# A hybrid decoder layer on one core: for twelve weight chunks of the down projection a DMA makes the low part

## The chip, the cores and the metric

The kernel runs on one core of a Trainium2 chip. A core has TensorE for matrix products, VectorE (DVE in the profile), ScalarE (ACT) and GpSimd (POOL) for elementwise work, SyncE (SP), which here only issues loads, and sixteen DMA engines that all queues share. The engines run side by side, each works through its own instructions in order, and they wait for each other through semaphores. The metric is the time of the whole program on the device in microseconds; lower is better.

## The reference

One layer works on 256 tokens of width 2048: a mixer of two recurrent branches, cross-attention, and a gated feed-forward network with a short causal convolution. The change concerns the last product of it, the down projection from 8192 to 2048.

```python
def conv_glu_ffn(h, w_up, conv_w, conv_b, w_down):
    u = h @ w_up
    uc = conv_b + sum(conv_w[j] * shift_right(u, CONV_WIDTH - 1 - j) for j in range(CONV_WIDTH))
    gate, up = split_cols(uc, (D_FF, D_FF))
    return (jax.nn.gelu(gate, approximate=True) * up) @ w_down
...
    x = x + rms_norm(y, mix_post_norm[l])
...
    x = x + rms_norm(cross_attention(h, m, xattn_wq[l], xattn_wkv[l], xattn_wo[l]), xattn_post_norm[l])
    h = rms_norm(x, ffn_pre_norm[l])
    x = x + rms_norm(conv_glu_ffn(h, ffn_w_up[l], ffn_conv_w[l], ffn_conv_b[l], ffn_w_down[l]), ffn_post_norm[l])
```

All inputs and the result are float32.

## The kernel before

**Split products.** TensorE reads its operands as `float32r`, which keeps fewer bits than float32. So each float32 matrix is split into a high part, the value rounded to `float32r`, and a low part, the value minus the high part, and a product becomes three: x high by w high, x low by w high, x high by w low. Splitting a weight chunk takes a cast by ScalarE (`wh`, line 448 in `Feed.hi`) and a subtraction by VectorE (`wl = raw - wh`, line 520 in `Feed.lo`).

**Chunks and buffers.** A weight chunk is 512 KB: 128 partitions by 1024 float32. `Feed` lists the chunks of all blocks in the order of their use (`src`). `dma` loads them with SP's queue into `raw` tiles (four buffers), `hi` makes `wh` tiles and `lo` makes `wl` tiles (five buffers each). A buffer comes free when the last reader of its earlier contents is done: for `raw` that is the subtraction, for `wh` and `wl` the matmuls of the chunk five places earlier.

**The down projection** is two blocks of kind `tm`, one for each half of the 2048 output columns, with 64 chunks each. A chunk holds 128 of the 8192 inputs and 1024 output columns. It is multiplied into four PSUM banks of 128 tokens by 512 columns, which makes 4 x 3 = 12 matmuls, by `tm_products` (line 524): for each bank the three products one after the other. The activations are split too (`as`, in `asplit`): a ScalarE cast and a VectorE subtraction for every two chunks.

**Pairs.** At six places of each block (`SEVEN`: 12, 20, 30, 38, 48, 56 and 10, 18, 28, 36, 46, 54) two chunks k and k + 1 are multiplied together by a scheme with seven block products in place of eight, so 21 matmuls in place of 24 (`seven_products`). Their weights have buffers of their own (`sraw`, loaded by `pair_loads`), and sums of the blocks are prepared in small steps in the six chunks before (`prepare`, `ahead_of_pairs`). The step of the loop that does a pair sets `skip`, so the loop runs no step for chunk k + 1.

**The order** of every engine's instructions is written out by `run`/`work`. In the step of chunk i it first makes sure of the splits up to `i + 1` (`feed.lo(i + 1 + pair)`), calls the activations' split (`b["xs"](k)`), then the splits up to `i + 3`, the loads up to `i + 7`, and then issues the matmuls of chunk i. `side.half()` gives other work, such as the evaluation of a finished block, its turn on VectorE and ScalarE. POOL has nothing to do in the down projection until its last microseconds.

Of the kernel before, what the change touches and what calls it, by code (L numbers as in the profile page):

```python
# [11 lines left out]
AF = mybir.ActivationFunctionType  # L12
ALU = mybir.AluOpType
AX = mybir.AxisListType

P = 128
# [138 lines left out]
def _layer(ctx, tc, nc, d, dbg):  # L155
    act, dve = Meter(nc.scalar, 200.0, 0.83), Meter(nc.vector, 130.0, 1.04)
    pool, pe, sp = nc.gpsimd, nc.tensor, nc.sync
# [32 lines left out]
    def mm(out, lhsT, rhs, start=True, stop=True):  # L190
        pe.matmul(out, lhsT, rhs, start=start, stop=stop, skip_group_check=True)  # L191
# [63 lines left out]
    def turns(ap):  # L255

        return ap.rearrange("p (a b) -> p b a", a=2)
# [25 lines left out]
    class Stat:  # L283


        def __init__(self, name, tag="ysb1", sq="au", home=None):
            self.name, self.tag, self.sq, self.home = name, tag, sq, home
            self.rc = cp.tile([P, 2], F32, name=name + "_c")
            self.n = 0
            self.done = False  # L290
# [89 lines left out]
    blocks = []  # L380
# [10 lines left out]
    class Feed:  # L391
        def __init__(self):
            a, g = blocks[0]["srcs"], blocks[1]["srcs"]
            self.src = a[:LEAD] + [c for p in zip(a[LEAD:], g) for c in p] + g[len(a) - LEAD:]
            self.src += [s for b in blocks[2:] for s in b["srcs"]]
            n, self.pairs, self.preps = sum(len(b["srcs"]) for b in blocks[:2]), {}, []
            for b in blocks[2:]:
                if b["seven"]:
                    for k in b["seven"]["at"]:
                        self.pairs[n + k], self.pairs[n + k + 1] = 0, 1  # L400
                        self.preps.append([n + k - 6, self.prepare(n + k, k), n + k, []])
                n += len(b["srcs"])
            self.raw, self.st, self.nd, self.ns, self.nl, self.nop = {}, {}, 0, 0, 0, 0
# [38 lines left out]
        def hi(self, upto):  # L442
            while self.ns <= min(upto, len(self.src) - 1):
                self.dma(self.ns)
                r = self.raw[self.ns]
                wh = self.staged("wh", r)
                for o, v in self.pieces(self.ns, wh, r):
                    nc.scalar.copy(o, v)  # L448
                self.st[self.ns] = [wh, None]
                self.ns += 1  # L450

        def prepare(self, c, k):
# [61 lines left out]
        def lo(self, upto):  # L514
            self.hi(upto)
            while self.nl <= min(upto, len(self.src) - 1):
                r = self.raw.pop(self.nl)
                wl = self.staged("wl", r)
                for o, v, h in self.pieces(self.nl, wl, r, self.st[self.nl][0]):
                    nc.vector.tensor_sub(o, v, h)  # L520
                self.st[self.nl][1] = wl
                self.nl += 1

    def tm_products(o, t, c, wx, first, last):
        wh, wl, xh, xl = wx
        t = slice(t // P * P, t // P * P + P)
        wh, wl = (turns(w[:, c:c + 512]) for w in (wh, wl))
        mm(o, xh[:, t], wh, start=first, stop=False)
        mm(o, xl[:, t], wh, start=False, stop=False)
        mm(o, xh[:, t], wl, start=False, stop=last)  # L530

    def seven_products(b, banks, ci, w0h, w0l, w1h, w1l):
        sv = b["seven"]
# [35 lines left out]
    def run():  # L569
        feed = Feed()  # L570
# [3 lines left out]
        i = 0  # L574
        pend = []

        def work(b):
# [6 lines left out]
            if b["wide"]:  # L584
                banks = [b["pool"]("fm", [P, 2, S]) for _ in range(nm)]
            elif b["kind"] == "fm":
                banks = [b["pool"]("fm", [P, 2, S]) for _ in range((nm + 1) // 2 * (1 + b["two"]))]
            else:
                banks = [b["pool"]("tm")[:, 0:min(b["cols"], 512)] for _ in range(2 * -(-b["cols"] // 512))]
            nk = sum(s.shape[1] for s in b["srcs"]) // (1 + b["two"])  # L590
            k = 0
# [4 lines left out]
            for ci, s in enumerate(b["srcs"]):  # L596
                if skip:
                    skip = False
                    continue
                join = b["seven"] and ci - b["seven"]["at"][-1]  # L600
                second = b["two"] and ci % 2
                if second:
                    k -= s.shape[1]
                if b["pre"]:
                    b["pre"](ci, feed)
                pair = 1 if b["seven"] and ci in b["seven"]["at"] else 0
                feed.lo(i + 1 + pair)
                side.half(True)
                side.more = lambda: feed.hi(i + 2)
                ahead = b["xs"](k)  # L610
                if b["seven"]:
                    feed.pair_loads(i)
                feed.lo(i + 3 + pair)
                feed.dma(i + 7 + pair)
                if b["seven"]:
                    feed.ahead_of_pairs(i)
                if b["seven"]:
                    if join >= 2:
                        if join == 2:
                            b["seven"]["joins"] = join_sums(b["seven"])  # L620
                        next(b["seven"]["joins"], None)
                wh, wl = feed.st.pop(i)
                later = []
                if b["seven"] and ci in b["seven"]["at"]:
                    seven_products(b, banks, ci, wh, wl, *feed.st.pop(i + 1))
                    k, i, skip = k + 2, i + 2, True
                    yield
                    continue
                for kj in range(s.shape[1]):
                    xh, xl = b["xs"](k) if kj else ahead  # L630
                    first, last = k == 0, k == nk - 1
                    if b["wide"]:
                        xw = b["xw"](k).rearrange("p h (a b) -> p h b a", a=2)
                        for m in range(nm):
                            a, c = (w[:, kj, m * P:(m + 1) * P] for w in (wh, wl))
                            mm(banks[m].rearrange("p h s -> p (h s)"), a, xw, start=first, stop=False)
                            mm(banks[m][:, 0], c, turns(xh), start=False, stop=last)
                    elif b["kind"] == "fm":
                        xh, xl = turns(xh), turns(xl)
                        for m in range(nm):  # L640
                            r = min(P, b["cols"] - m * P)
                            o = banks[second * 2 + m // 2][0:r, m % 2]
                            a, c = (w[:, kj, m * P:m * P + r] for w in (wh, wl))
                            mm(o, a, xh, start=(first and m % 2 == 0), stop=False)
                            if not (b["two"] and ci == 0):
                                mm(o, a, xl, start=False, stop=False)
                            mm(o, c, xh, start=False, stop=last)
                        if b["two"] and ci == 0:
                            later.append((kj, xl))
                        for j, v in later if len(later) == s.shape[1] else ():  # L650
                            for m in range(nm):
                                mm(banks[m // 2][:, m % 2], wh[:, j, m * P:(m + 1) * P], v, start=False, stop=False)
                    elif b["cols"] < 512:
                        a, c = (turns(w[:, kj]) for w in (wh, wl))
                        for v, w in ((xh, a), (xl, a), (xh, c)):
                            for t, o in enumerate(banks):
                                mm(o, v[:, t * P:(t + 1) * P], w, start=first and v is xh and w is a, stop=last and w is c)
                    else:
                        for g, o in enumerate(banks):
                            tm_products(o, g * P * 512 // b["cols"], g * 512 % b["cols"], (wh[:, kj], wl[:, kj], xh, xl),  # L660
                                        first, last)
                            if len(banks) == 4 and g == 1:
                                side.half()
                    k += 1
                    if kj + 1 < s.shape[1] and (not b["wide"] or kj % 2):
                        side.half()
                i += 1
                if ci < len(b["srcs"]) - 1:
                    yield
            if nt:  # L670
# [14 lines left out]
                if b["bankwise"]:  # L685
                    banks = banks[:-1] + [[aux("fm", [P, S]) for _ in range(2)]]
                for g, o in enumerate(banks):
                    by_tile = b["bankwise"] and g == len(banks) - 1
                    for m in range(2 if by_tile else 0):
                        for si, (w, kj, xh, xl) in enumerate(steps):  # L690
                            a, c = (v[:, kj, (g * 2 + m) * P:(g * 2 + m + 1) * P] for v in w)
# [4 lines left out]
                    for si, (w, kj, xh, xl) in enumerate(() if by_tile else steps):  # L696
# [3 lines left out]
                        for m in range(2 if b["kind"] == "fm" else 0):  # L700
                            a, c = (v[:, kj, (g * 2 + m) * P:(g * 2 + m + 1) * P] for v in w)
# [155 lines left out]
    cols = cp.tile([P, 8, 4], F32, name="cols")  # L857
# [841 lines left out]
    for b in range(2, 8):  # L1699
        block("fm", W("w_mw", b - 2), mo_xs, y_evac(b, sty, "z1", "postg", True), before=load_x if b == 2 else None,  # L1700
              cols=256, wide=mgp)
# [465 lines left out]
```

## Time and profile before

| | us |
|---|---|
| median of 3 runs | 1797.09 (1797.02 to 1797.45) |
| the profiled execution, its own time | 1796.52 |
| its span, first to last instruction | 1794.7 |
| TensorE, loading of weights | 1629.7 busy |
| ScalarE busy | 1076.7 |
| loads on SP's queue | 347.38 MB, 61.3% of 16 DMA engines |

The span is the time between the first and the last instruction of the profiled execution; some 1.8 us of its own time lie outside it. An engine's busy time is the sum of its instructions, and tells nothing of which of them sets the end: for that the profile follows the chain of work back from the last instruction. In the rows of the timeline the first two numbers are the start and the length in microseconds; then come the engine, the line, the operation, the tile written and the tiles read, and how many like instructions were merged. Lines of a DMA issue give the number of issues, the size, and the median time from issue to landing. A matmul's row lasts longer than the distance to the next one, as matmuls are pipelined. The down projection's matmuls run from 1462.9 us to 1786.9 us of the span.

### The profile page before, as it was taken

The numbers are of one execution on the slowest core, as the hardware profiler recorded it, in microseconds if no ns is written. First come the engines' busy times: TensorE is split into PE (matmuls) and PEld (weight loads), VectorE is DVE, ScalarE is ACT, GpSimd is POOL, SyncE is SP. The second block draws the span as 40 slices with busy tenths as digits, with TensorE's granted clock in tenths as the row PEclk, the third lists the DMA queues.
The fourth block names the chain that finished last, engine by engine and source line by source line (L and its number), as shares of the span: only waits on it lengthen the run. The fifth ranks groups of instructions, "written<-read, shape, count | busy, mean of one in ns | idle before, by whom it ended". The sixth has DMA issues, their size and how long they took to land.

```text
span 1794.7 us, 30098 instructions
## 1 busy us (share of the span) xinstructions
PE 1785.2 (99%) x11778; PEld 1629.7 (91%) x11778; DVE 1395.6 (78%) x2020; ACT 1076.7 (60%) x1616; POOL 28.9 (2%) x51
## 2 busy tenths in 40 slices
PE   9999999999999999999999999999999999999998
PEld 9999988888888999999999999999999998888887
DVE  7869995766665767778878777877777778888887
ACT  7576454654554666677566667666655655556554
POOL 0100000000100000000000000000000000000000
PEclk9999999999999999999999999999999999999999
DMA  8755564454556676656666666666666676767664
GB/s 283 206 170 186 164 190 146 125 180 144 200 188 211 227 243 186 190 150 197 208 203 198 203 209 192 199 206 204 199 200 209 192 229 213 227 186 227 209 209 129
DMA packets 99134, 351.59 MB, mean 196 GB/s; under 512 B 10896, under 2 KB 13968, under 8 KB 98864
## 3 DMA queue, kind: packets, MB, share of 16 engines
q1 hardware_dynamic: 97888, 347.38, 61.3%
q8 instruction: 92, 1.51, 0.3%
q0 software_dynamic: 384, 1.18, 0.2%
q10 hardware_dynamic: 720, 1.12, 0.2%
q14 instruction: 50, 0.41, 0.1%
HBM read 347.01 MB, written 2.10 MB: 195 GB/s over the span
## 4 chain that ended last, share of the span: by engine, by line
PE 99%; DVE 0%; DMA 0%; ACT 0%; issue 0%; SPq 0%; DVEq 0%; ACTq 0%
PE fm L191 55%; PE tm L191 37%; PE more L191 2%; PE gram L191 0%; PE Y L191 0%; PE lv L191 0%; DMA op<-in_op_dram 0%; PE X L191 0%; PE num L191 0%; PE zwa L191 0%; PE U L191 0%; PE gramA L191 0%; PE xo L191 0%; PE zg L191 0%; PE Tn L191 0%; PE mT L1472 0%
## 5 line engine op out<-in xcount | busy, mean ns | idle before, releaser
L520 DVE TENSOR_TENSOR wl<-raw,wh 128x1024 fp32r<-128x1024 f32 (+1 forms) x617 | 741.5, 1218 | 128.6 <-ACT wh L448 125.9
L448 ACT CAST wh<-raw 128x1024 fp32r<-128x1024 f32 (+1 forms) x617 | 633.6, 1044 | 112.7 <-PE tm L191 61.7
L191 PE MATMUL fm<-fx,wh 128*128 128x512 f32 (+1 forms) x2240 | 672.8, 364 | 0.6 <-DVE fx L68 0.4
L191 PE MATMUL fm<-fx,wl 128*128 128x256 f32 x2048 | 558.3, 273 | 0.0
L191 PEld LDWEIGHTS fm<-fx,wh 128*128 128x128 f32 x2240 | 409.3, 190 | 49.9 <-DVE fx L68 1.0
L191 PEld LDWEIGHTS fm<-fx,wl 128*128 128x128 f32 x2048 | 393.3, 192 | 0.0
L191 PE MATMUL tm<-wh,as 128*128 128x512 f32 x856 | 254.8, 379 | 0.0
L191 PE MATMUL tm<-wh,hx 128*128 128x512 f32 (+1 forms) x832 | 243.9, 378 | 1.4 <-ACT hx L68 1.4
L191 PEld LDWEIGHTS tm<-wh,as 128*128 128x128 f32 x856 | 161.7, 189 | 23.2 <-DVE as L68 0.3
L68 ACT COPY ul<-fm 128x256 f32<-128x256 f32 x128 | 44.9, 373 | 225.5 <-PE fm L191 225.5
L191 PE MATMUL fm<-hx,wh 128*128 128x256 f32 x1024 | 174.5, 277 | 0.0
L191 PEld LDWEIGHTS tm<-wh,hx 128*128 128x128 f32 x832 | 151.0, 189 | 21.8 <-POOL wh L507 1.6
L191 PE MATMUL tm<-wl,as 128*128 128x512 f32 x428 | 162.2, 379 | 0.0
L191 PEld LDWEIGHTS fm<-hx,wh 128*128 128x128 f32 x1024 | 155.6, 192 | 1.1
L191 PE MATMUL tm<-wl,hx 128*128 128x512 f32 (+1 forms) x416 | 152.5, 373 | 0.4 <-DVE wl L520 0.3
L68 DVE TENSOR_TENSOR us<-fm,ul 128x256 f32<-128x256 f32 x128 | 48.5, 420 | 131.2 <-ACT ul L68 131.2
L191 PE MATMUL fm<-hx,wl 128*128 128x256 f32 x512 | 140.8, 275 | 0.0
L68 ACT CAST as<-ac 128x512 fp32r<-128x512 f32 x64 | 39.4, 617 | 118.8 <-PE tm L191 118.8
L191 PEld LDWEIGHTS fm<-hx,wl 128*128 128x128 f32 x512 | 98.3, 192 | 0.0
L191 PEld LDWEIGHTS tm<-wl,as 128*128 128x128 f32 x428 | 80.9, 189 | 11.5
L191 PEld LDWEIGHTS tm<-wl,hx 128*128 128x128 f32 x416 | 77.5, 189 | 11.2 <-DVE wl L520 0.5
L191 PE MATMUL fm<-mg,wh 128*128 128x512 f32 (+1 forms) x320 | 84.9, 340 | 0.0
(406 smaller groups left out, 2114.8 us busy)
## 6 DMA issues: line engine op xcount, KB each, us to landing
raw<-in_w_fw_dram SPq DMA_DIRECT2D x232, 512.0 KB, 4.3
raw<-in_w_in_dram SPq DMA_DIRECT2D x160, 512.0 KB, 3.7
raw<-in_w_fd_dram SPq DMA_DIRECT2D x104, 512.0 KB, 4.1
raw<-in_w_br_dram SPq DMA_DIRECT2D x32, 512.0 KB, 4.2
raw<-in_w_mw_dram SPq DMA_DIRECT2D x24, 512.0 KB, 4.8
raw<-in_w_fu_dram SPq DMA_DIRECT2D x24, 512.0 KB, 4.0
end<-in_w_fd_dram SPq DMA_DIRECT2D x24, 512.0 KB, 3.6
raw<-in_w_mo_dram SPq DMA_DIRECT2D x8, 512.0 KB, 4.1
```

The lines of the kernel that those rows point to most:

```text
L68: return f(out, *a, **k)
L191: pe.matmul(out, lhsT, rhs, start=start, stop=stop, skip_group_check=True)
L448: nc.scalar.copy(o, v)
L520: nc.vector.tensor_sub(o, v, h)
```

## The change

For the chunk three places ahead of each pair, twelve in all (9, 17, 27, 35, 45, 53 of the first block, 7, 15, 25, 33, 43, 51 of the second), `wl` is made in another way. After the cast that makes `wh`, ScalarE writes `-raw`, rounded to `float32r`, which is minus the high part, into the `wl` tile, and a DMA issued by POOL adds the weights from memory onto it (`accum_op=ALU.add`). The subtraction of line 520 is left out for these chunks, and their `raw` tile is released by ScalarE. In the step four chunks ahead, `work` calls `lo(i + 3)` and `hi(i + 4)`, which makes the two parts of such a chunk a step earlier. And in such a chunk TensorE first does the two products with `wh` for all four banks, and then the product with `wl` for all four.

```diff
-            n, self.pairs, self.preps = sum(len(b["srcs"]) for b in blocks[:2]), {}, []
+            n, self.pairs, self.preps, self.added = sum(len(b["srcs"]) for b in blocks[:2]), {}, [], set()
...
                     for k in b["seven"]["at"]:
                         self.pairs[n + k], self.pairs[n + k + 1] = 0, 1
+                        self.added.add(n + k - 3)
...
                 self.st[self.ns] = [wh, None]
+                if self.ns in self.added:
+                    wl = self.st[self.ns][1] = self.staged("wl", r)
+                    nc.scalar.activation(wl, self.raw.pop(self.ns), AF.Copy, scale=-1.0)
+                    pool.dma_start(wl, self.src[self.ns], accum_op=ALU.add)
                 self.ns += 1
...
             while self.nl <= min(upto, len(self.src) - 1):
+                if self.nl in self.added:
+                    self.nl += 1
+                    continue
...
-        mm(o, xh[:, t], wh, start=first, stop=False)
-        mm(o, xl[:, t], wh, start=False, stop=False)
-        mm(o, xh[:, t], wl, start=False, stop=last)
+        if which > 1:
+            mm(o, xh[:, t], wh, start=first, stop=False)
+            mm(o, xl[:, t], wh, start=False, stop=False)
+        if which % 2:
+            mm(o, xh[:, t], wl, start=False, stop=last)
...
                     feed.pair_loads(i)
+                    if i + 4 in feed.added:
+                        feed.lo(i + 3)
+                        feed.hi(i + 4)
                 feed.lo(i + 3 + pair)
...
+                        late = i in feed.added
                         for g, o in enumerate(banks):
                             tm_products(o, g * P * 512 // b["cols"], g * 512 % b["cols"], (wh[:, kj], wl[:, kj], xh, xl),
-                                        first, last)
+                                        first, last, 2 if late else 3)
                             if len(banks) == 4 and g == 1:
                                 side.half()
+                        for g, o in enumerate(banks if late else ()):
+                            tm_products(o, g * P * 512 // b["cols"], g * 512 % b["cols"], (wh[:, kj], wl[:, kj], xh, xl),
+                                        first, last, 1)
```

More of the change, by code (lines that the diff above doesn't have):

```diff
@@ L522, in lo, with tm_products @@
                 self.nl += 1
-    def tm_products(o, t, c, wx, first, last):
+    def tm_products(o, t, c, wx, first, last, which=3):
         wh, wl, xh, xl = wx
```

## The prediction, made before the changed kernel ran

> **What bounds the kernel now.** I read the page's head, its busy table and its chain of work first.
>
> ```profile
> span 1794.7 us, 30098 instructions
> PE 1785.2 (99%) x11778; PEld 1629.7 (91%) x11778; DVE 1395.6 (78%) x2020; ACT 1076.7 (60%) x1616; POOL 28.9 (2%) x51
> ...
> PE 99%; DVE 0%; DMA 0%; ACT 0%; issue 0%; SPq 0%; DVEq 0%; ACTq 0%
> ```
>
> The path to the end is TensorE from start to finish; VectorE, which the change relieves, is on none of it by a whole per cent. Shares over the span can hide a stage, so I went to the stage that the change touches, the down projection (first matmul at 1462.9 us). The view by windows gives busy time per engine in two stretches of it, then the clock, the DMA share and GB/s; the view of waits, taken for the stage alone, says who waited there.
>
> ```profile
> 1462.00:1610.00 148.00, 148.00 (x689) 129.66 (x689) 124.21 (x155) 87.62 (x111) 0.00 (x0) 1.00 0.68 215
> 1610.00:1787.00 177.00, 177.00 (x821) 154.77 (x820) 152.15 (x192) 103.38 (x136) 0.55 (x1) 1.00 0.62 195
> ...
> ACT as L68 <- PE tm L191: 118.8, 61, 2.7
> DVE as L68 <- ACT as L68: 27.8, 20, 1.9
> DVE wl L520 <- ACT wh L448: 13.6, 57, 0.3
> ...
> PEld tm L191 <- DVE as L68: 0.3, 1, 0.3
> ```
>
> TensorE is busy 148.00 of 148 us and 177.00 of 177 us, at the full clock, and in the whole stage it waits for VectorE once, for 0.3 us. A busy matmul row alone would not prove that the array never idles, so I checked spacing: in the rows of the next fence chunk 14 of the first half starts at 1498.54 and chunk 17 at 1506.31, that is 36 matmuls in 7.77 us, or 0.216 us each and **2.59 us a chunk**. VectorE (124 of 148 us) and ScalarE (88 of 148 us) run ahead; ScalarE waits 118.8 us for TensorE to release the buffers of `as`. So there is nothing in this stage that a faster VectorE could give to the end: at most that 0.3 us.
>
> **What is removed.** Twelve subtractions of line 520, at 1218 ns by the page's row, 14.6 us of VectorE. All of it lies beside TensorE, so it is worth 0.
>
> ```profile
> L520 DVE TENSOR_TENSOR wl<-raw,wh 128x1024 fp32r<-128x1024 f32 (+1 forms) x617 | 741.5, 1218 | 128.6 <-ACT wh L448 125.9
> L448 ACT CAST wh<-raw 128x1024 fp32r<-128x1024 f32 (+1 forms) x617 | 633.6, 1044 | 112.7 <-PE tm L191 61.7
> ```
>
> **What is reordered.** In an added chunk TensorE does its eight products with the high part first and its four with the low part last. The count of matmuls and weight loads stays 12 and 12, and the trace shows the same 0.216 us whichever product follows which, so 0. VectorE and ScalarE keep their side work: the half step still stands between the same banks.
>
> **What is added.** Per chunk: one ScalarE pass over 128x1024 for the negative (I take the cast's 1044 ns), one DMA of 512 KB issued by POOL, and one wait of TensorE's ninth matmul of that chunk for the DMA's landing. Behind that waiting matmul is everything on TensorE, so whatever the DMA is late goes to the end one for one. ScalarE's 12 x 1.04 = 12.5 us fall into its waits for TensorE. The rows below (start, length, engine, idle before) give the places: first TensorE, then ScalarE around chunk 17 and around the step where chunk 9 will be prepared.
>
> ```profile
> 1498.54 0.59 PE L191 MATMUL tm<-wh,as 128*128 128x512 f32 x2
> ...
> 1506.31 0.59 PE L191 MATMUL tm<-wh,as 128*128 128x512 f32 x2
> ...
> 1508.03 0.38 PE L191 MATMUL tm<-wl,as 128*128 128x512 f32 x1
> ...
> 1486.23 0.59 PE L191 MATMUL tm<-wh,as 128*128 128x512 f32 x2
> ...
> 1498.73 0.62 ACT L68 CAST as<-ac 128x512 fp32r<-128x512 f32 x1 [1.97 <-PE tm L191]
> 1499.26 1.99 ACT L448 CAST wh<-raw 128x1024 fp32r<-128x1024 f32 x2
> 1503.91 0.62 ACT L68 CAST as<-ac 128x512 fp32r<-128x512 f32 x1 [2.67 <-PE tm L191]
> ...
> 1474.01 1.99 ACT L448 CAST wh<-raw 128x1024 fp32r<-128x1024 f32 x2
> 1478.66 0.62 ACT L68 CAST as<-ac 128x512 fp32r<-128x512 f32 x1 [2.67 <-PE tm L191]
> ```
>
> The early call (`i + 4 in feed.added`) is reached only in steps that the loop runs. For a pair at k the step is k - 7, and for 20, 30 -> 23, 38 -> 31 and so on that is the second half of an earlier pair (13, 31, 49; 11, 29, 47) in six of the twelve cases, where `skip` jumps over it. Those six chunks (17, 35, 53; 15, 33, 51) are prepared by the ordinary `lo(i + 3)`, three chunks ahead; the other six (9, 27, 45; 7, 25, 43) four ahead.
>
> **Short lead, chunk 17.** Its cast starts at 1499.26; the two casts in that row end at 1501.25, and the negative takes the second one's place, so it ends there. It needs no buffer that is still held: the low tile of chunk 12 was read before chunk 14 began. The displaced cast of chunk 18 moves by 1 us into the idle 2.67 us before 1503.91. From a ScalarE end to a POOL DMA there are 0.31 us in the trace (77.72 + 1.04 = 78.76, issue at 79.07):
>
> ```profile
> 77.72 1.04 ACT L68 CAST uh<-up 64x1024 fp32r<-64x1024 f32 x1
> 79.07 0.52 POOL L831 DMA_DIRECT2D uh<-uh  x1 [1.59 <-ACT uh L68]
> ```
>
> Issue at 1501.56; the ninth matmul of chunk 17 is due at 1508.03 (the row above: eight spacings after 1506.31). **The DMA has 6.47 us to land.**
>
> **Long lead, chunk 9.** The cast cannot start before chunk 4 has left TensorE (five `wh` buffers): 1486.23 - 4 x 2.59 = 1475.87. ScalarE is free at 1476.00, so cast and negative end near 1478.0, inside the 2.67 us of idle before 1478.66; issue 1478.3, due 1486.23 + 1.73 = 1487.96: **9.66 us**. If ScalarE's cover were gone, the `as` casts would slip by a microsecond, and they have a whole pair, 5.18 us, before TensorE reads them: still 0.
>
> **How long the adding DMA takes.** No run shows one. The nearest rows: 512 KB loads on SP's queue, POOL's own copies, the stage's load on the DMA engines, and one transfer of 1 MB.
>
> ```profile
> raw<-in_w_fd_dram SPq DMA_DIRECT2D x104, 512.0 KB, 4.1
> ...
> end<-in_fpg_dram SPq DMA_DIRECT2D x1, 1024.0 KB, 6.7
> uh<-uh POOLq DMA_DIRECT2D x2, 256.0 KB, 4.9
> gup<-in_g_up_dram POOLq DMA_DIRECT2D x2, 256.0 KB, 3.9
> ...
> 1456.00:1794.70 338.70, 333.01 (x1548) 290.30 (x1546) 285.58 (x360) 196.78 (x257) 0.55 (x1) 1.00 0.65 204
> ```
>
> The last row: 204 GB/s at a share of 0.65, so 314 GB/s at full use, 0.83 us per 256 KB. POOL's 256 KB copies land in 3.9 and 4.9 us, 4.4 between. The add has to fetch the weights (512 KB) and the old contents of the tile (512 KB), 768 KB more than the copy: 3 x 0.83 = 2.5 us, together **6.9 us**. Lower end, if the old contents cost nothing: 3.9 + 0.83 = 4.7. Upper end: 4.9 + 2.5 plus one 512 KB load of SP served in between (1.67), 9.1; and by the 1 MB row, 6.7 us on SP plus POOL's slower start (4.9 against SP's 4.1 for half the bytes), 7.5 or more. An operation unlike any in the trace may lie beyond 9.1.
>
> The Trainium skill has a rule that speaks against the change: "Collectives: The Full Stack", section "The bandwidth ceiling: the fold count and why AG ≠ RS ≠ AR", says that an adding transfer reads two sources through the same queue and so runs at half the rate of a copy. No run here shows that rule; by it the add would be the second rival below, at its lower end.
>
> **The sum.** Six short chunks late by 6.9 - 6.47 = 0.43 us: 2.6 us. Six long ones in time with 2.8 us over: 0. Removed 0, reordered 0, ScalarE 0. The profiled execution took 1796.52 us (1.8 of it outside the span of 1794.7), so 1799.1; the median of the runs shown, 1797.09, is 0.57 above it: **1799.7 us**, 0.14% slower than before. A measurement of this kernel tells about 0.2%, 3.6 us, from no change; that is lateness of 0.6 us in each short chunk, a landing at 7.07 us. So "no change that can be told" holds for any landing up to 7.07 us, and the forecast is close to that edge.
>
> **Rivals.**
> 1. *In time everywhere.* Landing at 6.47 us or less (down to the lower end, 4.7): 1797.1. For it: POOL's four 256 KB copies are all near 4 to 5 us, and the deferral gives the DMA 1.73 us more than a plain product order. Also the case if, against my reading, the early call reached all twelve. It shares the forecast's verdict.
> 2. *The wait takes the place of the subtraction, slower.* Place: the ninth matmul of chunks 17, 35, 53, 15, 33, 51. It decides from a landing of 7.07 us. At 7.5 us it is 6 x 1.03 = 6.2 us, 1803.3; at 9.1 us 6 x 2.63 = 15.8 us, 1812.9. For it: the DMA engines are 65% taken in this stage by the weights of the next chunks, and SP's load of chunk 23 is released by the very negative that starts this DMA, as they share a `raw` buffer.
> 3. *The add is far dearer than a copy.* Above 9.66 us the long chunks stall too: at 12 us 6 x 5.53 + 6 x 2.34 = 47 us, 1844. Nothing in the trace speaks for it but that no such transfer is in it.
> 4. *A relieved VectorE helps.* It would need TensorE to wait for it in this stage, and that is the one row of 0.3 us; over 0.2% faster has no place in the profile.
>
> **How the numbers follow.** Forecast and rival 1 together, landing up to 7.07 us: 0.50 (0.30 in time, 0.20 slightly late). Rival 2: 0.36. Rival 3: 0.11. Rival 4, or something of the profile that I misread: 0.03. Faster 0.03, same 0.50, slower 0.47. The range leaves out rival 3 and the top of rival 2: from 1796.4, nothing late and the spread of the runs, to 1812, a landing near 9.0 us (6 x 2.5 = 15).
>
> **What would show it.** Twelve POOL DMAs into `wl` with a landing near 6.9 us; TensorE rows idle before a `wl` product in chunks 17, 35, 53, 15, 33, 51 and none in the other six; ScalarE's wait for TensorE before `as` down by some 12 us; VectorE's stage total down by 14.6. Wrong if the landing differs by a microsecond, if the long-lead chunks stall too, or if all twelve have the same lead.

## The result and the profile after

| | us |
|---|---|
| before, median | 1797.05 (1796.51 to 1797.45, 4 runs) |
| changed, median | 1810.86 (1808.48 to 1812.48, 4 runs) |
| ratio | 1.0077, 95% interval 1.0063 to 1.009 |
| profiled execution of the changed kernel | 1812.48, its span 1810.7 |

The change makes the kernel **slower by 13.8 us**, 0.77%. The time lies close to the upper end of the range on record (1812; the slowest of the four runs is beyond it) and 11 us from the point, 1799.7. What came true is the second rival: the wait for the adding DMA takes the place of the subtraction.

First the page of the changed kernel: the head, the busy table, the DMA queue of POOL, the chain of work, the row of the subtractions (the code has moved, line 520 is now 528), and the DMA issues with the median time to landing.

```profile
span 1810.7 us, 30122 instructions
...
PE 1789.7 (99%) x11778; PEld 1630.2 (90%) x11778; DVE 1383.0 (76%) x2008; ACT 1088.0 (60%) x1628; POOL 39.1 (2%) x63
...
q0 software_dynamic: 2112, 7.47, 2.1%
...
PE 8%; DMA 3%; ACT 1%; issue 0%; DVE 0%; DVEq 0%; ACTq 0%
...
L528 DVE TENSOR_TENSOR wl<-raw,wh 128x1024 fp32r<-128x1024 f32 (+1 forms) x605 | 727.2, 1218 | 133.3 <-ACT wh L449 131.1
...
raw<-in_w_fd_dram SPq DMA_DIRECT2D x104, 512.0 KB, 4.4
...
wl<-in_w_fd_dram POOLq DMA_DIRECT2D x12, 512.0 KB, 8.9
```

Twelve subtractions are gone (617 to 605, 14.3 us of VectorE by that row), and a link appears in the chain that was not there: DMA, 3% of the span. (The shares of this chain add up to an eighth of the span; the profile follows it no further back.) The adding DMA takes **8.9 us** from issue to landing; the forecast had 6.9. SP's own loads of these weights are slower too, 4.4 us in place of 4.1.

The view of waits for the down projection says who paid (columns: total, times, longest). Below it stand two POOL rows of the timeline, one for chunk 9 and one for chunk 17, and TensorE's rows at chunk 17.

```profile
ACT as L68 <- PE tm L191: 123.2, 60, 4.0
...
PEld tm L191 <- DMA wl<-in_w_fd_dram: 15.5, 11, 2.5
PE tm L191 <- DMA wl<-in_w_fd_dram: 11.3, 7, 2.1
...
1478.31 0.95 POOL L454 DMA_DIRECT2D wl<-in_w_fd_dram  x1 [833.13 <-ACT wl L453]
1502.04 0.87 POOL L454 DMA_DIRECT2D wl<-in_w_fd_dram  x1 [22.79 <-ACT wl L453]
...
1506.78 1.89 PE L191 MATMUL tm<-wh,as 128*128 128x512 f32 x8
1510.66 0.92 PE L191 MATMUL tm<-wl,as 128*128 128x512 f32 x3 [1.99 <-DMA wl<-in_w_fd_dram]
```

Here the change is seen at work. Eight high products run, then the array waits, and the ninth matmul starts at 1510.66, 0.04 us after the DMA of chunk 17 has landed (issue 1502.04, landing 8.57 us later in the trace). The spacing of TensorE's matmuls, summed over the stage, accounts for the 16.0 us by which the spans differ (this execution is the slowest of the four):

| gaps beyond the 0.216 us spacing | us |
|---|---|
| at the ninth matmul of chunks 17, 35, 53, 15, 33, 51 | 2.15, 2.22, 1.42, 1.78, 2.30, 1.51: 11.4 |
| the same in chunks 9, 27, 45, 7, 25, 43 | 0.28, 0, 0.02, 1.07, 0, 0.24: 1.6 |
| eight matmuls at half the clock after the gap in chunk 35 | 1.8 |
| 0.1 us in the second matmul after a wait, nine times | 0.9 |
| sum (the time behind the last matmul is 0.2 us longer than before) | 15.7 |

The six chunks that were read as having the short lead have seven tenths of the loss.

### The profile page after: what moved, and what is told of

It is laid out like the page before. It is cut to its first block, busy times and chain, and to the rows that moved or that the text cites. A ratio compares the mean times of both kernels' runs of the same rounds, so it can differ in the third digit from the quotient of the medians.

```text
span 1810.7 us, 30122 instructions
## 1 busy us (share of the span) xinstructions
PE 1789.7 (99%) x11778; PEld 1630.2 (90%) x11778; DVE 1383.0 (76%) x2008; ACT 1088.0 (60%) x1628; POOL 39.1 (2%) x63
## 3 DMA queue, kind: packets, MB, share of 16 engines
q8 instruction: 92, 1.51, 0.3%
## 5 line engine op out<-in xcount | busy, mean ns | idle before, releaser
L528 DVE TENSOR_TENSOR wl<-raw,wh 128x1024 fp32r<-128x1024 f32 (+1 forms) x605 | 727.2, 1218 | 133.3 <-ACT wh L449 131.1
L191 PE MATMUL tm<-wh,as 128*128 128x512 f32 x856 | 249.6, 380 | 0.0
L68 ACT CAST as<-ac 128x512 fp32r<-128x512 f32 x64 | 39.4, 617 | 123.2 <-PE tm L191 123.2
L68 DVE TENSOR_TENSOR as<-ac,as 128x512 fp32r<-128x512 f32 x64 | 44.2, 692 | 54.4 <-ACT as L68 52.5
```

Of the source, the lines that this page charges most:

```text
L68: return f(out, *a, **k)
```

## The experiments

The theory after the result: TensorE pays one for one what the landing exceeds the lead; the landing is long because an add reads two operands for each row, **and** because it stands behind SP's loads that were issued just before it. The rivals: the rearrangement of the products and steps costs by itself; or VectorE's work holds up POOL's preparation of the transfer.

### The order alone

The changed kernel without the negative and without the adding DMA; `lo` makes all low parts.

```diff
-                if self.ns in self.added:
-                    wl = self.st[self.ns][1] = self.staged("wl", r)
-                    nc.scalar.activation(wl, self.raw.pop(self.ns), AF.Copy, scale=-1.0)
-                    pool.dma_start(wl, self.src[self.ns], accum_op=ALU.add)
...
-                if self.nl in self.added:
-                    self.nl += 1
-                    continue
```

> The order and the early steps of the change are kept, VectorE makes all low parts again, and no DMA adds. Theory (the loss is TensorE's wait for the adding DMA's landing): no gap before a wl product, 1797.0 us, within 0.6 of before. Rival (the new product order, or ScalarE's cast a step earlier, costs by itself): some 1804 to 1811 us, with gaps at the twelve chunks.

Measured: 1796.58 us, ratio 0.9999 (0.999 to 1.0009). No gap before a `wl` product. The new order of the products and the early steps cost nothing, so that rival is gone.

### A copy in place of the add

```diff
-                    pool.dma_start(wl, self.src[self.ns], accum_op=ALU.add)
+                    pool.dma_start(wl, self.src[self.ns])
```

> The DMA copies the weights over the negative instead of adding them, so the low part is not subtracted and holds the whole weight. Theory (each 4 KB row takes 328 ns because the add reads two operands): rows near 160 ns, landing shorter by 8 rows x 0.16 = 1.3 us, so short-lead chunks near 7.0 us (8.3 in the changed kernel) and 0.5 us late each, long-lead ones near 8.4 and in time: 1797 + 6 x 0.55 = 1800 to 1802 us. Rival (the reads do not matter, the late first packet does): landing within 0.3 us of the changed kernel's, 1809 to 1811 us.

Measured: 1796.86 us, ratio 1.0002 (0.9993 to 1.0012), below both ranges that were expected. The negative, the POOL issue, the wait and 6 MB more traffic are all there and cost nothing that the runs can tell; in the profiled run one chunk, 51, still waits for 0.9 us. The view by tile of POOL's DMAs gives minimum, median and maximum to the landing, first here, then in the changed kernel:

```profile
DMA to landing us min/median/max: 5.0/7.4/7.7
```
```profile
DMA to landing us min/median/max: 7.9/8.9/10.0
```

The median 4 KB row takes 174 ns here and 328 ns in the changed kernel, by the packets of the two traces. That agrees with what the Trainium skill's "Collectives: The Full Stack", section "The bandwidth ceiling: the fold count and why AG ≠ RS ≠ AR", says of the reduce step of a collective, that the add needs two source reads. The landing shrank by more than I expected: in the short-lead chunks to 5.0 to 5.5 us (one 7.4), from 7.9 to 8.7. Eight rows on each DMA engine explain 1.2 us of those 3. The single transfers below show the same: the add is 1.7 us slower than the copy when both run alone, and 3.3 us slower when one load of SP goes ahead of each. Why a load in front costs the add more than the copy was not tried.

### Only the long leads

```diff
-                        self.added.add(n + k - 3)
+                        if k - 8 not in b["seven"]["at"]:
+                            self.added.add(n + k - 3)
```

> Only the six chunks whose early call is reached (four ahead) keep the adding DMA. Theory (a chunk costs what its landing exceeds its lead): the gaps of those six in the changed kernel's trace, 0.4 + 0 + 0 + 1.2 + 0.1 + 0.3 = 2.0 us, so 1799 us. Rival (every adding DMA costs alike, by its traffic): half of the loss, 1804 us.

Measured: 1798.23 us, ratio 1.0011 (1.0001 to 1.002). With half of the adding DMAs a ninth of the loss is left. So the number of adding DMAs is not what sets the loss: the six with the long lead cost little, as the gaps of the changed kernel had said.

### The negative from wh

```diff
-                    nc.scalar.activation(wl, self.raw.pop(self.ns), AF.Copy, scale=-1.0)
+                    self.raw.pop(self.ns)
+                    nc.scalar.activation(wl, wh, AF.Copy, scale=-1.0)
```

> ScalarE makes the negative from the wh tile and not from the raw tile, so raw is released about 1 us earlier and SyncE's next load starts 1 us earlier against the adding DMA. Theory (the add's first packet waits until the loads that SyncE issued just before have been served): first packet and landing some 0.9 us earlier in the short-lead chunks, 7.4 us in place of 8.3, 1803 to 1806 us. Rival (POOL's own preparation is what delays the first packet, held up by VectorE's work): landing unchanged, 1810 us.

Measured: 1802.54 us, ratio 1.0036 (1.0023 to 1.0049); a spread of 1800.12 to 1806.34 in 5 runs, the profiled one the fastest. That is just below the range expected. One microsecond between a load of SP and the adding DMA, with the same work and the same bytes, takes back 8 of the 14 us. In the short-lead chunks the first packet comes 1.6 to 1.8 us after the issue (2.3 to 3.3 in the changed kernel), and four of six land in 5.8 to 6.2 us; the other two take 6.7 and 8.1.

```profile
DMA to landing us min/median/max: 5.8/7.8/9.4
```

### The added chunk two places ahead

Chunk k - 2 in place of k - 3, so that the step four chunks ahead is never the skipped half of a pair.

```diff
-                        self.added.add(n + k - 3)
+                        self.added.add(n + k - 2)
```

> The added chunk is the one two places ahead of its pair instead of three, so that the step four chunks ahead exists for all twelve. Theory (lead against landing): the lead is some 9.3 us for all twelve, landings stay between 8 and 10 us, so late by 0 to 0.6 us: 1797 to 1801 us, with no gap over 1.5 us. Rival (the loss does not hang on the lead): 1809 to 1812 us.

Measured: 1800.32 us, ratio 1.002 (1.001 to 1.0029); the largest gap is 0.96 us.

```profile
DMA to landing us min/median/max: 7.4/8.0/9.0
```

The time is as expected, but my lead was wrong: it is 8.1 us, not 9.3. POOL issues chunk 18's add at 1502.82, and its ninth matmul, which does not wait in this run, starts at 1510.92. In such a step ScalarE first makes `as` and the casts of two chunks. So a median landing nearly fills the lead, and four of the twelve are late, by up to a microsecond.

### The same, with the negative from wh

> As the run before it, and the negative is made from the wh tile. Theory: lead near 9.3 us, landing shorter by up to a microsecond as in the run that negated wh three ahead; no chunk late: 1796.7 to 1798 us. Rival (the loads of SyncE before the adding DMA are more in this place and eat the lead): 1800 us or more.

Measured: 1799.12 us, ratio 1.0014 (1.0005 to 1.0024). A miss: three landings, of 8.3 to 9.5 us, are still late, and the gain against the run before it is not clear of the noise. The last two loads in front of an add now go out 1.37 and 0.95 us before it (0.94 and 0.28 in the run before), so both are still in front of it.

### The plain product order

```diff
-                        late = i in feed.added
+                        late = False
```

> The changed kernel with the products of an added chunk in the plain order, high, high, low for each bank: the first low product is the third matmul and not the ninth, 6 x 0.216 = 1.3 us earlier. Theory (whatever the DMA is late goes to the end one for one): each of twelve waits grows by 1.3 us where it was late before, the long-lead ones by 0.9 to 1.3: 1822 to 1827 us. Rival (TensorE's queue hides part of it): under 1818 us.

Measured: 1830.86 us (1825.3 to 1832.88, 4 runs), ratio 1.0184 (1.0167 to 1.0202). Its due points are 1.3 us earlier, and all twelve wait. The six short-lead landings happen to be 0.54 us shorter on average than in the changed kernel, and their waits are 0.75 us longer: together the 1.3 us.

```profile
PEld tm L191 <- DMA wl<-in_w_fd_dram: 25.5, 12, 4.1
```

So no queue of TensorE hides any of it. The time is 4 us beyond the expected range. The half clock after long gaps adds to it: three times in the profiled run, 5 us in all, and that run is the fastest of the four (a mean granted clock of 0.997, and 0.994 in the other three).

### Single transfers

A program that does nothing of the layer but single 512 KB DMAs of POOL, one at a time.

> Leaves out the whole computation but the loading of some weight chunks: single DMAs of 512 KB issued by POOL one at a time, with nothing beside them, with one or three SyncE loads of 512 KB issued just before, or with eight VectorE additions running. Theory (two reads for each row, and a place behind the loads already issued): alone, rows of 160 to 175 ns for the copy and 328 ns for the add, landing 4.5 to 5.3 us for the copy and 5.8 to 6.5 for the add; behind one load 1 to 1.6 us more, behind three 3 to 5 us more; beside VectorE's additions as alone, within 0.3 us. Rival (VectorE holds up POOL's preparation): the add beside VectorE lands 1 us or more later than alone, and the loads matter less.

The view of DMA issues, taken for eight of the twelve stretches in order of time: a copy alone; an add alone; an add with one SP load issued 0.27 us before (its own line first); an add with three SP loads (issued 0.27 us before it, and 0.15 and 0.63 us after POOL has begun to issue it); an add alone, with a ScalarE copy waiting for it; an add beside VectorE's additions; a copy behind one load; a copy behind three loads, with the program's output stores beside it.

```profile
wl<-in_w_fd_dram POOLq DMA_DIRECT2D x1, 512.0 KB, 3.7
...
wl<-in_w_fd_dram POOLq DMA_DIRECT2D x1, 512.0 KB, 5.5
...
ra<-in_w_fd_dram SPq DMA_DIRECT2D x1, 512.0 KB, 3.8
wl<-in_w_fd_dram POOLq DMA_DIRECT2D x1, 512.0 KB, 7.8
...
wl<-in_w_fd_dram POOLq DMA_DIRECT2D x1, 512.0 KB, 8.9
...
wl<-in_w_fd_dram POOLq DMA_DIRECT2D x1, 512.0 KB, 5.3
...
wl<-in_w_fd_dram POOLq DMA_DIRECT2D x1, 512.0 KB, 5.3
...
wl<-in_w_fd_dram POOLq DMA_DIRECT2D x1, 512.0 KB, 4.5
...
wl<-in_w_fd_dram POOLq DMA_DIRECT2D x1, 512.0 KB, 7.9
```

Alone, an add costs 1.7 us more than a copy. One load in front makes the add 2.3 us later (the copy 0.8), three make it 3.4 us later. Beside VectorE's additions it lands as alone, so that rival is gone. Two of the sizes expected were wrong: alone, both the copy and the add land sooner than expected, and one load in front costs more than the 1 to 1.6 us. In the packets of the trace the first one of an add follows its issue by 1.6 us alone, by 2.5 to 3.0 behind one load and by 4.2 to 4.3 with three. So a later start is 0.9 to 1.4 of the 2.3 us that one load costs; where the rest arises was not tried. The first packets of the changed kernel are of the same two kinds: 2.3 to 3.3 us in the short-lead chunks, with one load released by the negative itself, and 4.1 to 4.6 in the long-lead ones, with two or three.

### Holding the raw tile

A tiny ScalarE copy of the added chunk's `raw` tile, behind the cast of the chunk after it, keeps the tile, and so the load that waits for it, until after the adding DMA is issued.

```diff
                 self.st[self.ns] = [wh, None]
+                if self.held is not None:
+                    nc.scalar.copy(end3, self.held[:, 0, 0:1])
+                    self.held = None
                 if self.ns in self.added:
+                    self.held = r
```

> The changed kernel, with the raw tile of an added chunk held by one more tiny ScalarE copy (128x1) behind the cast of the chunk after it, so that the SyncE load which that tile releases is issued after the adding DMA and not 0.28 us before it. Theory (the add waits behind loads already issued, and pays for each of them): first packet of the short-lead chunks near 1.6 us in place of 2.3 to 3.3, landing 6 to 7 us in place of 8.3, so 0 to 0.5 us late each; the long-lead chunks lose one of three loads ahead of them and are in time: 1797.5 to 1802 us. Rival (negating from wh helped for another reason than the order of the DMAs): landing and time as in the changed kernel, 1809 to 1812 us.

Measured: 1799.19 us, ratio 1.0013 (1.0003 to 1.0023). In every short-lead chunk the first packet now comes 1.6 us after the issue, and five of six land in 6.3 to 6.6 us; the sixth takes 8.1. The load at stake is issued 0.75 us after the add of chunk 17 in place of 0.28 before, and but for the tiny copy nothing else is changed. Waits of 2.8 us are left in the profiled run, 1.6 of them in the chunk of that sixth landing.

```profile
DMA to landing us min/median/max: 6.3/7.2/9.3
```

### Both mended

> Both: the added chunk two places ahead of its pair, so that all twelve are prepared four chunks ahead, and its raw tile held by one more tiny copy. Theory: lead 9.3 us, landing under 8 us for all: no wait for the DMA, 1796.5 to 1797.5 us, and no faster than before, as TensorE has no gap to give. Rival (some landing still falls behind other loads): 1798 to 1800 us as without the hold.

The head, the busy table and the chain of work of this run, ScalarE's wait for TensorE, and the landings of POOL's DMAs:

```profile
span 1795.1 us, 30133 instructions
...
PE 1785.6 (99%) x11778; PEld 1630.6 (91%) x11778; DVE 1383.5 (77%) x2008; ACT 1089.2 (61%) x1640; POOL 39.1 (2%) x63
...
PE 99%; DVE 0%; DMA 0%; ACT 0%; issue 0%; DVEq 0%; ACTq 0%
...
ACT as L68 <- PE tm L191: 107.2, 61, 2.7
...
DMA to landing us min/median/max: 6.2/7.0/7.9
```

Measured: 1796.93 us, ratio 1.0002 (0.9992 to 1.0011). One load in place of two goes out in the microsecond before each add. All twelve land within their 8.1 us, TensorE has no gap before a `wl` product, and the whole loss is gone with the twelve adding DMAs in place. VectorE's busy time stays 12 us lower than before, and the time is that of before and not less. No version here is faster than the kernel before, and in this stage the profile shows no gap of TensorE from which a gain could come.

## Why the prediction came out as it did

- **What bounds the kernel: right.** No kernel here is measurably faster than before. Relieving VectorE of 12 subtractions is worth nothing, as the last experiment shows with the wait removed.
- **The reorder and ScalarE's negative at 0: right.** The order alone and the copy both run at the time of before.
- **Which chunks have which lead: right.** The early call misses six chunks. Issue was expected at 1501.56 for chunk 17 and 1478.3 for chunk 9; it came at 1502.04 and 1478.31. At chunk 17 TensorE too is 0.48 us later than before (0.39 of it from the wait in chunk 9), so the lead is the 6.47 us that was worked out.
- **The landing: mis-sized, and that is the step that failed.** The forecast took 4.4 us for a 256 KB copy and added 2.5 us for 768 KB more. It came to 6.9; measured were 7.9 to 8.7 us in the short-lead chunks and 9.2 to 10.0 in the long. The bytes were sized well: the second read of 512 KB was put at 1.67 us, and the add alone is 1.7 us slower than the copy alone. The base was not a quiet copy: POOL's copies of 3.9 us ran beside three SP loads (464 to 472 us of the span before, median landing 5.7), and alone even 512 KB take only 3.7 us. So 6.9 was 1.5 us above the add alone and still too short. What the sum put at nothing is SP's load directly in front of the add, 2.3 us in the single transfers; with that load held back, five of the six short-lead landings fell to 6.3 to 6.6 us. That load stood in the upper end only, at 1.67 us, though the same text named the reason to expect it every time: the negative that starts the add also releases the `raw` tile for SP's next load. An event that has a fixed place in each step belongs in the sum.
- **One for one onto the end: right**, with two riders that were not in the sum. A wait costs 0.1 us more in the second matmul after it, and a wait can be followed by half the clock (1.8 us, once). The short-lead waits alone make 11.4 us; that the total still falls inside the range, near the edge that was drawn for a landing of 9.0 us in the short-lead chunks, is in part luck.
- **The long-lead chunks in time: nearly.** Their lead of 9.66 us met landings of 9.2 to 10.0; 1.6 us of loss, 1.07 of it in the second half's chunk 7. Two or three loads are in front of them. The text had named a landing off by a microsecond and a stall of the long-lead chunks as signs of being wrong, and both came.
- **ScalarE's wait for TensorE** went up, from 118.8 to 123.2 us, and not down by 12. The negatives did use that idle time, but TensorE's own 16 us of waiting came back into it: 118.8 - 12.5 + 16 = 122.3. In the last kernel, where TensorE does not wait, it is 107.2, down by the 12 that were forecast. VectorE's total fell by 12.6 us in the changed kernel, not by 14.6.
- **The likeliest case was the wrong one.** It was decided by 0.6 us of landing, and the upper end for the landing, 9.1 us, was nearer to the 7.9 to 8.7 us measured than the 6.9 of the sum.

## What to carry to other kernels

An engine that the chain of work does not pass through is worth no relief that puts a new wait before the engine it does pass through; if it must be done, price the wait from issue to landing, with the loads that will be in flight at that place, and not from a transfer elsewhere in the kernel. Look which instruction releases the buffer of the next load: where the same instruction also starts the urgent transfer, the load can get in front of it, and holding the buffer a microsecond longer keeps it behind; here that took back 11.7 of the 13.8 us. And check that an early step written for chunk i exists in a loop that skips some i.

## What the runs showed of the hardware that was not expected

**In these runs the queues are served in something near the order of issue.** A 512 KB load of SP issued 0.27 us before an add on POOL's queue moves the add's first packet from 1.6 us to between 2.5 and 3.0 us and its landing from 5.3 to 5.5 us to 7.7 to 7.8, while that load itself lands in 3.8 us (such a load was not run alone; the median in the kernel before is 4.1). The Trainium skill's "DMA: Bandwidth & Descriptors", section "Issuing engines are not separate DMA queues", says that DMAs of several engines interleave on the same DMA engines; here they do once both have started (with three loads, the packets of the third run beside the add's), but the load issued first is hardly slowed.

**Half the clock after a wait.** The view by windows around chunk 35 of the changed kernel, before the wait, after it and after that; the eighth value is the granted clock.

```profile
1556.00:1558.20 2.20, 0.25 (x2) 0.00 (x0) 1.73 (x3) 0.48 (x1) 0.00 (x0) 1.00 0.84 248
1558.30:1561.70 3.40, 3.39 (x8) 2.77 (x9) 0.60 (x1) 1.25 (x2) 0.00 (x0) 0.51 0.77 283
1561.80:1564.00 2.20, 2.20 (x12) 1.91 (x11) 1.96 (x2) 1.68 (x3) 0.00 (x0) 1.00 0.00 0
```

A wait of 2.2 us was followed by 3.4 us at half the clock: eight matmuls in the time of sixteen. A wait of 2.3 us in chunk 33 was not. In the kernel with the plain order waits of 2.8, 3.8 and 2.2 us were followed by it and waits of 2.6 and 2.5 us were not, so the length alone does not decide. The clock records of the traces say more. Each such stretch lasts 3.41 us, and the three of the plain order start at 1511.13, 1562.33 and 1613.53 us, 51.20 us or fifteen stretches apart; so they fit a grid of 3.41 us. (In the changed kernel the next stretch, at the program's end, starts 73 such steps after the one at chunk 35.) In the grid interval that ends where a stretch starts, TensorE was idle for 2.62, 3.30 and 2.07 us, and for 2.06 us in the changed kernel. In every other interval of the down projection in these two traces it was idle for at most 1.91 us. So the idle time within one interval fits all of these waits; no run was made to test it.
